# mLSTM input projection: the low halves of sixteen weight blocks formed on the vector engine instead of GpSimd

## The chip, the cores and the metric

The kernel runs on one core of one Trainium2 chip. The metric is the device time of one execution in microseconds; the shown time of the kernel before is the median of 3 runs, 1545.17 us (1545.28, 1542.12 and 1545.17). The engines of the core each run their own in-order queue of instructions: TensorE (PE in the profile, with its weight loads under PEld), the vector engine (DVE), the scalar engine (ACT), GpSimd (POOL) and SyncE (SP, which only issues transfers).

## The reference

Two layers of a backbone work on 1024 latent tokens and 128 context tokens of width 1024. Layer 0 runs four mLSTM heads in both directions beside grouped-query attention, from one input projection; layer 1 is neighbourhood attention. Only the projection of layer 0 and the mLSTM heads matter here:

```python
p = jnp.einsum('btd,dn->btn', h, w_in)
qa, ka, va, oa, gates, qb, kb, vb, z = jnp.split(p, offsets(EVEN_SIZES), axis=-1)
...
h_f, C_f, n_f, m_f = mlstm_scan(qa, ka, va, ig_f, fg_f, *st_fwd)
h_b, C_b, n_b, m_b = mlstm_scan(rev(qa), rev(ka), rev(va), rev(ig_b), rev(fg_b), *st_bwd)
ha = rmsnorm(h_f + rev(h_b), g_hn.reshape(H_A, 1, DH_A)) * jax.nn.sigmoid(oa.astype(jnp.float32))
...
y = jnp.concatenate([ha, from_heads(hb)], axis=-1) * jax.nn.silu(z)
```

Each head has five column blocks of 128 in `w_in`: q, k, v, o and z.

## The kernel before

All products with float32 weights are done as three products of a reduced-width type. A weight block `raw` (128 x 1024, eight 128 x 128 tiles side by side) is loaded by SP, ACT rounds it to the high part `whi` (line 114), and the low part is the difference `wlo = raw - whi` (line 115, in the helper `split`). `feat` then multiplies a block with one chunk of 384 tokens: 24 matmuls (8 tiles, and for each `whi` with the high activations, `whi` with the low ones, `wlo` with the high ones: lines 366 to 368) that add up in one bank of PSUM. The banks of this kind (`pj`) are two. When a chunk is done its bank is emptied by ACT or DVE: q and v by copies (`qT`, `vT`, lines 101 and 103), k by ACT (line 584), o by ACT (lines 603 and 604), z by ACT and DVE (lines 390 and 391, then 610).

Four blocks of head 0 are projected in the front of the kernel, while the inputs are normalised. Their low parts are formed on DVE already. The sixteen others pass through `blocks`, which calls `weights` and `feat` block by block: the z block of head 0, and q, k, v, o and z of heads 1 to 3. `blocks` runs between the pieces of the mLSTM heads, so that TensorE has projections of the next head to do while one head's chain goes on. That chain is: state updates (`kw` on ACT line 662, the product in the single bank `o` line 665, the update of the state tiles `cs` on DVE line 672), the decay matrices `e` (ACT line 649, GpSimd line 650, DVE lines 698 and 703), the products with values and states (lines 709 and 711), the norm of the result (ACT 717, DVE 720 and 721, ACT 724, DVE 725, ACT 728, GpSimd lines 133 and 134, ACT 732), the transposes on TensorE (line 106) and the gate on DVE (line 743).

Between these the generator `rest` (`mods_rest`) computes the modulation vectors of the later sub-layers on DVE: 32 loads `wm` of 512 KB and for each four multiply-and-sum instructions (`mj<-wm,cb`, line 253, 128 x 512), 128 in all.

The order of the instructions on each engine is not the order of the code: the program is built with a scheduler that plays the program through a timeline of its own and places each instruction when its operands would be ready there (`schedule_with_timeline_sim=True`, line 1628). Only in the attention stages is TensorE's order fixed by hand. After that each engine's queue is fixed and runs in order, an instruction waiting at the head of its queue holds up all behind it.

Of the kernel before, what the change touches and what calls it, by code (L numbers as in the profile page):

```python
# [39 lines left out]
class Kern:  # L40
# [1246 lines left out]
    def run(self):  # L1287
        nc, a = self.nc, self.a
# [2 lines left out]

        def blocks(hd, evs, bs, new=None):
            for b in bs:
                w = self.weights(a["w_ab"][5 * hd + b], new=new)
                for c in range(NC):
                    self.feat(h, w, evs[b], [c])
                    next(rest, None)

        with self.phase("front"):
# [21 lines left out]
            w = [[self.u([P, NB, 256], F32R, n) for n in ("whi", "wlo")] for _ in range(4)]  # L1321
# [52 lines left out]
        with self.phase("a"):  # L1374
            self.gates(gT)
            self.c0 = [self.load_c0(hd) for hd in range(2)]
            self.nall = self.const([P, 8], "nall")
            later(2, (1, 2))
            for b in range(3, NB + 1):
                for c in (1, 2):  # L1380
                    later(c, (b,))
            blocks(0, evs, (4,), lambda n: self.t(n, 1, [P, D], F32R))
            nxt, evs = self.mlstm_proj(1)
            blocks(1, evs, (0, 1))
        with self.phase("mlstm", ("e", 3, [P, 4, CW])):
            self.ts = [self.decays_load(0, g) for g in range(NC)]
            start = self.mlstm_start(0)
            rest = self.mods_rest()
            for hd in range(HA):
                self.mlstm(hd, *start, *pr())  # L1390
                if hd < HA - 1:
                    pr = nxt
                    blocks(hd + 1, evs, (2, 3, 4))
                    start = self.mlstm_start(hd + 1)
                    if hd < HA - 2:
                        nxt, evs = self.mlstm_proj(hd + 2)
                        blocks(hd + 2, evs, (0, 1))
            for _ in rest:
                pass
        with self.phase("g", ("nr", 3, [P, 3, 256])):  # L1400
            w = self.gqa_kv(h, self.zb(h))
            Q, early = [], []
            for g in range(2):
                q, w = self.gqa_q(h, g, w, Q, early)
                Q.append(q)
        gz, w = w, []
# [7 lines left out]
        with self.phase("out0"):  # L1414
            new = lambda: self.t("x", 5, [P, D])
# [32 lines left out]
        with self.phase("na"):  # L1448
# [12 lines left out]
            w, ys, gg = [], [], []  # L1461
# [170 lines left out]
```

## Time and profile before

| | |
|---|---|
| runs before | 1545.28, 1542.12, 1545.17 us; median 1545.17 |
| the profiled execution: its time | 1544.44 us |
| its span, first to last instruction | 1542.7 us |
| mean granted TensorE clock | 0.994 |
| PE busy in the span | 1497.6 us (97%) |
| DVE, ACT, POOL busy | 828.7, 711.1, 487.9 us |
| L115 on POOL, 128 x 1024 | 59 instructions, 145.2 us |
| stretch of the sixteen blocks | low parts formed from 71.0 to 348.7 us |

A row of the timeline gives the start in us from the span's start, the duration in us, the engine, the line, the operation, and output<-inputs by the program's names; in brackets stands how long the engine was idle just before, and whose instruction ended that. A row of the windows gives for each engine its busy time and number of instructions in a stretch, then the granted TensorE clock. A row for a tile or a line gives the least, the median and the greatest duration in ns.

### The profile page before, as it was taken

The page shows a single profiled execution, that of the slowest core. Times are in us where ns is not written, and L with a number is a line of the kernel's source. Part 1 is how long each engine was busy: PE and PEld are TensorE (multiplying, and loading weights), DVE is VectorE, ACT ScalarE, POOL GpSimd, SP SyncE. Part 2 cuts the span into 40 slices and gives each one's busy share as a digit, 9 for nine tenths or more (in the row PEclk, how much of TensorE's full clock was granted, in tenths as well). Part 3 has the DMA queues.
Part 4 walks back from the last instruction along what each step waited for, and adds up shares of the span by engine and source line. Part 5 has one row for each costly group of instructions (what it writes and reads, how often), then busy time and mean ns, then how long its engine had stood idle before and what let it go on. Part 6 is the DMA issues. An engine that isn't in the chain of part 4 may idle for free.

```text
span 1542.7 us, 27090 instructions
## 1 busy us (share of the span) xinstructions
PE 1497.6 (97%) x10139; PEld 1377.5 (89%) x10139; DVE 828.7 (54%) x2371; ACT 711.1 (46%) x1767; POOL 487.9 (32%) x660
## 2 busy tenths in 40 slices
PE   7899999999999899999999999999999999999998
PEld 5799999999999888877888989999999999989886
DVE  5832887954457756665465352435253434445532
ACT  4523524344435767777354352435253434445411
POOL 0102323221235745566123241233132323233200
PEclk9999999999999999999999999999999999999999
DMA  9203536422210000022334122131213021225342
GB/s 381 71 15 117 220 126 221 150 91 89 108 64 29 17 24 32 24 73 67 124 122 151 64 61 79 39 103 34 84 42 101 27 86 47 78 79 165 113 131 82
DMA packets 73284, 143.80 MB, mean 93 GB/s; under 512 B 15737, under 2 KB 44609, under 8 KB 73153
## 3 DMA queue, kind: packets, MB, share of 16 engines
q1 hardware_dynamic: 68566, 126.91, 24.6%
q10 hardware_dynamic: 4586, 15.16, 2.6%
q8 instruction: 80, 1.31, 0.3%
q14 instruction: 52, 0.42, 0.1%
HBM read 115.47 MB, written 21.86 MB: 89 GB/s over the span
## 4 chain that ended last, share of the span: by engine, by line
PE 87%; DVE 6%; ACT 2%; issue 2%; DMA 2%; POOL 1%; SPq 0%; DVEq 0%; POOLq 0%; ACTq 0%
PE pj L366 12%; PE pj L367 12%; PE pj L368 12%; PE pj L381 7%; PE pj L382 7%; PE pj L383 7%; PE s L907 4%; PE o L947 4%; PE ptr L106 4%; PE o L1282 4%; PE tr L106 3%; PE s L1259 3%; PE pj L106 2%; DVE mj L253 2%; DMA wm<-in_w_modT_dram 1%
## 5 line engine op out<-in xcount | busy, mean ns | idle before, releaser
L366 PE MATMUL pj<-hh,whi 128*128 128x384 f32 x1168 | 400.2, 343 | 4.4 <-DVE z L391 2.0
L368 PE MATMUL pj<-hh,wlo 128*128 128x384 f32 x1168 | 397.6, 341 | 0.0
L367 PE MATMUL pj<-hl,whi 128*128 128x384 f32 x1168 | 397.6, 340 | 0.0
L115 POOL TENSOR_TENSOR wlo<-raw,whi 128x1024 fp32r<-128x1024 f32 x59 | 145.2, 2464 | 302.9 <-ACT whi L114 241.8
L366 PEld LDWEIGHTS pj<-hh,whi 128*128 128x128 f32 x1168 | 220.5, 189 | 8.9 <-ACT qT L101 2.5
L367 PEld LDWEIGHTS pj<-hl,whi 128*128 128x128 f32 x1168 | 220.5, 189 | 1.2
L368 PEld LDWEIGHTS pj<-hh,wlo 128*128 128x128 f32 x1168 | 220.3, 189 | 1.0
L1269 POOL TENSOR_SCALAR sb<-sb,sm 128x512 f32<-128x512 f32 (+1 forms) x128 | 84.7, 666 | 246.2 <-DVE sm L1268 242.6
L917 POOL TENSOR_SCALAR pr<-pr,smg 128x384 f32<-128x384 f32 x192 | 109.3, 586 | 81.1 <-PE pj L106 41.5
L381 PE MATMUL pj<-whi,hh 128*128 128x256 f32 x432 | 122.4, 284 | 0.3 <-DVE nr L782 0.3
L382 PE MATMUL pj<-wlo,hh 128*128 128x256 f32 x432 | 122.4, 284 | 0.0
L383 PE MATMUL pj<-whi,hl 128*128 128x256 f32 x432 | 122.3, 283 | 0.0
L908 DVE CUSTOM_DVE_ANT_0 pr<-s,zero 128x384 f32<-128x384 f32 x192 | 103.4, 552 | 25.1 <-PE s L907 21.7
L381 PE MATMUL pj<-whi,yh 128*128 128x512 f32 x288 | 114.2, 397 | 1.5 <-DVE o L1077 1.5
L382 PE MATMUL pj<-wlo,yh 128*128 128x512 f32 x288 | 113.8, 395 | 0.0
L383 PE MATMUL pj<-whi,yl 128*128 128x512 f32 x288 | 113.4, 394 | 0.0
L1267 ACT ACTIVATE sb<-sb,sm 128x512 f32<-128x512 f32 (+1 forms) x128 | 88.9, 695 | 52.7 <-DVE sm L1265 49.1
L253 DVE CUSTOM_DVE_ANT_0 mj<-wm,cb 128x512 f32<-128x512 f32 x128 | 108.8, 850 | 4.1 <-DMA wm<-in_w_modT_dram 2.0
L907 PE MATMUL s<-Kst,Q 128*128 128x384 f32 x384 | 107.5, 371 | 0.7 <-DVE smg L908 0.7
L114 ACT CAST whi<-raw 128x1024 fp32r<-128x1024 f32 x77 | 79.7, 1045 | 19.5 <-DMA raw<-in_w_v_dram 6.7
L1265 DVE CUSTOM_DVE_ANT_1 sb<-s,bias 128x512 f32<-128x512 f32 (+1 forms) x112 | 72.9, 664 | 25.2 <-PE ptr L106 12.6
L381 PEld LDWEIGHTS pj<-whi,hh 128*128 128x128 f32 x432 | 81.3, 188 | 1.4 <-issue 0.5
(346 smaller groups left out, 2887.9 us busy)
## 6 DMA issues: line engine op xcount, KB each, us to landing
wm<-in_w_modT_dram SPq DMA_DIRECT2D x32, 512.0 KB, 5.9
raw<-in_w_c_dram SPq DMA_DIRECT2D x25, 512.0 KB, 3.5
raw<-in_w_ab_dram SPq DMA_DIRECT2D x20, 512.0 KB, 3.6
e<-rbd ACTq DMA_DIRECT2D x12, 768.0 KB, 6.5
bias<-in_na_bias_dram SPq DMA_DIRECT2D x16, 576.0 KB, 5.0
wm<-in_w_mod_dram SPq DMA_DIRECT2D x16, 512.0 KB, 10.0
raw<-in_w_out_dram SPq DMA_DIRECT2D x16, 512.0 KB, 3.5
y<-yd SPq DMA_DIRECT2D x18, 448.0 KB, 3.4
```

Source lines behind the costliest of these rows:

```text
L106: self.nc.tensor.transpose(out, in_, self.ident)
L115: (eng_lo or nc.gpsimd).tensor_tensor(lo, src, hi.bitcast(F32), ALU.subtract)
L253: nc.vector.tensor_tensor_reduce(junk, w[:, b, :], cb[:, r, :], 1.0, 0.0, ALU.mult, ALU.add, mp[:, hf, q // 4, 2 * (q % 4) + b, r : r + 1])
L366: nc.tensor.matmul(ps[:, :CW], a, hh, start=k == 0, stop=False)
L367: nc.tensor.matmul(ps[:, :CW], a, hl, start=False, stop=False)
L368: nc.tensor.matmul(ps[:, :CW], b, hh, start=False, stop=k == KB - 1)
L381: nc.tensor.matmul(ps[:, :width], hh, a, start=k == 0, stop=False)
L382: nc.tensor.matmul(ps[:, :width], hh, b, start=False, stop=False)
L383: nc.tensor.matmul(ps[:, :width], hl, a, start=False, stop=k == KB - 1)
L907: nc.tensor.matmul(s[:, :CW], x, y, start=part == 0, stop=part == 1)
L908: nc.vector.tensor_tensor_reduce(pr[:, c, :], s[:, :CW], zero, -1.0, -NEG, ALU.add, ALU.min, m3[:, c : c + 1])
L917: nc.gpsimd.tensor_scalar(pr[:, c, :], pr[:, c, :], r, 0.5, ALU.mult, ALU.mult)
```

## The change

`blocks` passes `"lo"` to `weights`, so that line 115 goes to DVE for the sixteen blocks that `blocks` handles. Other users of `split` are as they were. (The four blocks of z for the attention heads and the weights of later stages have their own calls.)

```diff
         def blocks(hd, evs, bs, new=None):
             for b in bs:
-                w = self.weights(a["w_ab"][5 * hd + b], new=new)
+                w = self.weights(a["w_ab"][5 * hd + b], "lo", new=new)
                 for c in range(NC):
                     self.feat(h, w, evs[b], [c])
                     next(rest, None)
```

As the scheduler sets the order anew, not only these sixteen instructions move. Three places show how.

First, DVE's queue where the front ends: the last low activations `hl` are done, the gates begin (`rows`, `line`), and the first of the sixteen blocks is prepared. `qT_577` empties the bank `pj_903` of head 0's q. Before and after in one piece:

```order
 L474 MEMSET line_772 1x8
 L477 COPY line_772<-sm_775 1x4 x2
+L115 TENSOR_TENSOR wlo_1100<-raw_1097,whi_1099 128x1024
 L103 COPY qT_577<-pj_903 128x2x16x8
 L414 TENSOR_TENSOR gT_165<-pj_744,cross_761 16x2x16x8
```

The low part now stands between the two small copies and the emptying of the bank.

Second, DVE's queue in the chain of state updates of head 1 (`cs_2003` and `cs_2004` are the two directions' states, `o_2271` and the like the products that they wait for, `wlo_2494` the low part of a block of head 2). Before:

```order
L672 SCALAR_TENSOR_TENSOR cs_2004<-cs_2004,astb,o_2263 128x129
L103 COPY k_2214<-ptr_2220 128x384
L253 ISA mj_1690,mp<-wm_2230,cb_1693 128x512
L253 ISA mp 128x1
L672 SCALAR_TENSOR_TENSOR cs_2003<-cs_2003,astb,o_2271 128x129
L672 SCALAR_TENSOR_TENSOR cs_2004<-cs_2004,astb,o_2271 128x129
L253 ISA mj_1690,mp<-wm_2230,cb_1693 128x512
```

With the change:

```order
L672 SCALAR_TENSOR_TENSOR cs_2003<-cs_2003,astb,o_2271 128x129
L672 SCALAR_TENSOR_TENSOR cs_2004<-cs_2004,astb,o_2271 128x129
L103 COPY k_2214<-ptr_2220 128x384
L115 TENSOR_TENSOR wlo_2494<-raw_2491,whi_2493 128x1024
L253 ISA mj_1690,mp<-wm_2230,cb_1693 128x512
L253 ISA mp 128x1
L672 SCALAR_TENSOR_TENSOR cs_2003<-cs_2003,astb,o_2279 128x129
```

The update that stood behind the first `mj` stands ahead of it, and the next update has the low part and one `mj` ahead of it.

Third, GpSimd's queue in head 1's norm (`sm_2357` and `sm_2417` are the reciprocal roots of two groups of chunks, `e_2363` the decay matrices of the next head):

```order
 L133 TENSOR_SCALAR sm_2357<-sm_2353 128x3
 L134 TENSOR_TENSOR sm_2357<-sm_2357,mhalf 128x3
-L650 AFFINE_SELECT e_2363<-e_2363 128x384
-L115 TENSOR_TENSOR wlo_2723<-raw_2720,whi_2722 128x1024
 L133 TENSOR_SCALAR sm_2417<-sm_2413 128x3
```

The second root follows the first without the low part (and without one of the two selections of the decay matrices, which went ahead) between them.

## The prediction

> **What bounds the kernel now.** I read the page first, then the windows over the stretch in which the sixteen blocks are prepared, then TensorE's waits there, and last the timeline around each of those waits.
>
> ```profile
> PE 1497.6 (97%) x10139; PEld 1377.5 (89%) x10139; DVE 828.7 (54%) x2371; ACT 711.1 (46%) x1767; POOL 487.9 (32%) x660
> ```
> ```profile
> 160.00:300.00 140.00, 134.36 (x842) 130.16 (x841) 123.48 (x324) 61.60 (x192) 44.88 (x41) 1.00 0.50 176
> 300.00:350.00 50.00, 49.96 (x330) 49.21 (x329) 32.44 (x93) 21.71 (x72) 13.21 (x13) 1.00 0.33 121
> 350.00:440.00 90.00, 90.00 (x588) 89.56 (x587) 34.89 (x89) 33.56 (x106) 16.36 (x29) 1.00 0.25 91
> ```
> TensorE bounds the kernel: it is busy for 97% of the span. The change can only win what TensorE idles or loses in clock in its stretch. From 160 to 300 us TensorE is idle for 140.00 - 134.36 = 5.6 us, and this is also where DVE is fullest, 123.5 of 140 us. From 300 to 440 us there is nothing left to win. Behind that, TensorE has no slack that would swallow a gain: what it wins here moves the end.
>
> ```profile
> PE pj L366 <- DVE z L391: 2.0, 2, 1.4
> PE pj L366 <- ACT qT L101: 2.0, 2, 1.6
> PE tr L106 <- ACT hs L732: 1.7, 2, 1.0
> PE s L711 <- DVE cs L672: 1.1, 1, 1.1
> PE o L665 <- DVE cs L672: 0.2, 1, 0.2
> ```
> These are TensorE's waits from 60 to 350 us. The longest six behind 150 us are two for z, one and one for the states cs, two for hs: 2.0 + 1.1 + 0.2 + 1.7 = 5.0 us. So I looked at what each of the late instructions stood behind.
>
> ```profile
> 279.85 2.91 POOL L115 TENSOR_TENSOR wlo<-raw,whi 128x1024 fp32r<-128x1024 f32 x1 [1.50 <-ACT whi L114]
> ...
> 280.84 2.47 DVE L253 CUSTOM_DVE_ANT_0 mj<-wm,cb 128x512 f32<-128x512 f32 x1
> ...
> 283.24 0.54 DVE L391 SCALAR_TENSOR_TENSOR z<-th,pj 128x384 f32<-128x384 f32 x1
> ...
> 283.84 0.44 PE L366 MATMUL pj<-hh,whi 128*128 128x384 f32 x1 [1.37 <-DVE z L391]
> ```
> ```profile
> 233.58 2.39 POOL L115 TENSOR_TENSOR wlo<-raw,whi 128x1024 fp32r<-128x1024 f32 x1 [21.21 <-ACT whi L114]
> ...
> 233.74 2.78 DVE L253 CUSTOM_DVE_ANT_0 mj<-wm,cb 128x512 f32<-128x512 f32 x1
> ...
> 236.45 0.60 DVE L672 SCALAR_TENSOR_TENSOR cs<-cs,astb,o 128x129 f32<-128x129 f32 x2
> 236.84 0.49 PE L711 MATMUL s<-cs,e 128*128 128x129 f32 x2 [1.09 <-DVE cs L672]
> ```
> This is the point of the case. Whenever GpSimd forms a low part, a multiply-and-sum of DVE that overlaps it takes 2.5 to 2.8 us and ends about half a us behind GpSimd's instruction. Its usual time is 0.69 us:
>
> ```profile
> L253 DVE CUSTOM_DVE_ANT_0 mj<-wm,cb x103: 643/691/2924, 159.9 to 299.5; 128x512 f32<-128x512 f32 x103
> L253 DVE CUSTOM_DVE_ANT_0 mj<-wm,cb 128x512 f32<-128x512 f32 x103 | 89.4, 868 | 3.6 <-DMA wm<-in_w_modT_dram 2.0
> L115 POOL TENSOR_TENSOR wlo<-raw,whi x9: 2386/2657/2941, 166.1 to 295.2; 128x1024 fp32r<-128x1024 f32 x9
> L115 DVE TENSOR_TENSOR wlo<-raw,whi x18: 1214/1224/1992, 19.5 to 1420.6; 128x1024 fp32r<-128x1024 f32 x18
> ```
> The first three rows are of 160 to 300 us, the last of the whole span. So DVE is not only busy there, it stands: 103 x (0.868 - 0.691) = 18.2 us of its 123.5 are spent in instructions that wait for GpSimd, and the z or the state behind them makes TensorE wait.
>
> The two waits for hs pass through GpSimd's own queue:
>
> ```profile
> 264.34 2.94 POOL L115 TENSOR_TENSOR wlo<-raw,whi 128x1024 fp32r<-128x1024 f32 x1 [4.70 <-ACT whi L114]
> ...
> 267.37 0.52 POOL L133 TENSOR_SCALAR sm<-sm 128x3 f32<-128x3 f32 x1
> ...
> 268.92 1.28 POOL L134 TENSOR_TENSOR sm<-sm,mhalf 128x3 f32<-128x3 f32 x1
> ...
> 270.23 0.99 ACT L732 ACTIVATE hs<-hs,sm 128x128 f32<-128x128 f32 x3 [2.84 <-POOL sm L134]
> ...
> 270.69 0.33 PE L106 MATMUL tr<-cc,hs 128*128 128x128 f32 x1 [0.96 <-ACT hs L732]
> ```
> The root of the norm stands behind a low part on GpSimd, ACT waits 2.84 us for it and TensorE 0.96.
>
> **The change part by part.** (1) *The first block, 71 to 75 us.*
>
> ```profile
> 71.02 3.21 POOL L115 TENSOR_TENSOR wlo<-raw,whi 128x1024 fp32r<-128x1024 f32 x1 [11.13 <-ACT whi L114]
> ...
> 72.07 2.18 DVE L477 COPY line<-sm 1x4 f32<-1x4 f32 x1
> ...
> 74.18 0.15 DVE L477 COPY line<-sm 1x4 f32<-1x4 f32 x1
> 74.25 0.41 DVE L103 COPY qT<-pj 128x256 f32<-128x256 f32 x1
> ...
> 74.69 0.27 ACT L101 COPY qT<-pj 128x128 f32<-128x128 f32 x1 [1.09 <-DVE qT L103]
> 75.00 0.45 PE L366 MATMUL pj<-hh,whi 128*128 128x384 f32 x1 [1.57 <-ACT qT L101]
> ```
> A copy of four numbers takes 2.18 us, because GpSimd is at its low part; the bank is emptied late and TensorE idles 1.57 us. With the change DVE does the two copies (its twin behind takes 0.15 us) from 72.07 to about 72.37, the low part until 73.59 (1.22 us; `whi` was ready by 71.02, when GpSimd began), and the bank at 73.59 instead of 74.25. TensorE starts 0.66 us earlier: **-0.7 us**, and its gap shrinks to 0.9.
>
> (2) *The clock.* Behind that gap TensorE loses half its clock:
>
> ```profile
> 72.67:76.09 3.42, 1.85 (x12) 1.25 (x11) 2.51 (x5) 0.74 (x2) 1.56 (x1) 1.00 0.22 40
> 76.09:82.91 6.82, 6.82 (x27) 6.31 (x27) 0.57 (x3) 0.00 (x0) 0.00 (x0) 0.50 0.14 57
> ```
> 6.82 us at 0.50 cost 3.4 us. The stretch ahead has TensorE busy for 1.85 of 3.42 us. The gap of 1.37 us at 283 us was not followed by a slower clock (the window above shows 1.00 from 160 to 300). With 0.9 us of gap I take the clock to stay full: **-3.4 us**; the bounds are 0 and -3.4. The three runs before, two near 1545.2 and one at 1542.1, are 3.1 us apart, which is near this price; so I count it as part of the median.
>
> [...]
>
> (3) *The nine blocks from 160 to 300 us.* DVE loses 18.2 us of standing and gains 9 x 1.22 = 11.0 us of work, each piece placed by the scheduler and half as long as the old stall. If TensorE's waits go with DVE's lost time, 7.2 of 18.2, or 40%, of the 5.0 us go: -2.0 us. If the waits came only because the stalls were long, all go: -5.0 us. A bank needs emptying while the other fills, and 24 matmuls take about 24 x 90.00/588 = 3.7 us by the row of 350 to 440 us; a low part and an `mj` ahead of a bank, 1.9 us, fit into that, and the old 2.8 us with what stood before them did not. At GpSimd the root loses 2.9 us of queue, but DVE's new low part can stand ahead of the norm's own steps. I take **-3.5 us**.
>
> (4) *The other six.*
>
> ```profile
> L115 POOL TENSOR_TENSOR wlo<-raw,whi x16: 2367/2490/3215, 71.0 to 346.3; 128x1024 fp32r<-128x1024 f32 x16
> ```
> Of the sixteen, one is the first block and nine are those of (3). Three of the others lie between 80 and 160 us and three behind 300 us, and TensorE's list of waits has next to nothing there: 6 x 1.22 = 7.3 us, half of it on a DVE that is idle 17.6 of 50 us from 300 to 350. **0**, covered by that idleness; without the cover at most 0.275 us of waiting per us (5.0/18.2), 2.0 us.
>
> (5) *What is queued behind.* Before, GpSimd waited for `whi` and nothing was hurt. Now DVE waits for it, with the emptying of banks and the state updates behind.
>
> ```profile
> 292.59 0.69 DVE L253 CUSTOM_DVE_ANT_0 mj<-wm,cb 128x512 f32<-128x512 f32 x1
> ...
> 294.10 1.03 ACT L114 CAST whi<-raw 128x1024 fp32r<-128x1024 f32 x1
> ...
> 298.35 0.55 DVE L103 COPY qT<-pj 128x384 f32<-128x384 f32 x1
> ```
> In the new order the low part of this block follows an `mj` that ended at 293.28, and `whi` was done at 295.13: a wait of 1.9 us. Behind it stands a bank of q that was emptied only at 298.35, so even here nothing is late: 295.13 + 1.22 + one `mj` of 0.7 is 297.1. I laid the other blocks onto the old times in the same way. The last, at 346 us, would wait for `whi` too, where TensorE has other work, and the one at 198 us would, but there the new order of ACT has the cast earlier. **0.** No transfer is added; the buffer `raw` is free 1.2 us sooner.
>
> The sum: -0.7 - 3.4 - 3.5 = -7.6 us. On the profiled execution (1544.44 us, span 1542.7 and 1.7 around it) that is 1536.8; the median of the runs is 0.7 higher, so **1537.5 us**.
>
> **The rivals.** *The clock stays slow* (0.20). For it: in the same span other gaps are followed by full clock and by half clock, so the tie between gap and clock rests on one place. Against: it starts within 1.1 us of the gap's end. Time: 1545.17 - 0.7 - 3.5 = 1541.0.
>
> *The waits come back* (0.15). DVE stays near full, the low parts stand ahead of z and the states, and TensorE waits as before, only elsewhere: 1545.17 - 0.7 - 3.4 = 1541.1 with the clock full, 1544.5 with it slow. For it: two thirds of the freed time is refilled. Against: pieces of 1.22 us instead of 2.8.
>
> *DVE waits for the casts: slower* (0.10). The low part is at the head of DVE's queue while ACT, with its own queue of norm and evacuation, has not rounded the block. If each of the nine waited 1.9 us as at 293 us, DVE would stand or work 9 x 3.1 = 28.1 us in place of 18.2; at 0.275 us per us TensorE waits 7.7 instead of 5.0, and a gap of over 1.57 us costs another 3.4 of clock: 1545.17 - 0.7 + 2.7 + 3.4 = 1550.6. It decides once the mean wait for `whi` is over 18.2/9 - 1.22 = 0.8 us. Against: the new order of ACT puts some of these casts earlier.
>
> **How the numbers follow.** The forecast has 0.55, the rivals 0.20, 0.15 and 0.10. About 0.2%, 3.1 us, is what a measurement of this kernel can tell from no change, so faster means under 1542.1. The forecast counts there in full, the slow clock (1541.0, spread 1.7) with 0.14, the returning waits with 0.05: faster 0.74. Same: 0.06 + 0.10 = 0.16. Slower 0.10. The forecast's own range is 1534 to 1541: all five us of waits gone is 1536.0, and another clock loss more or less is worth 1.7 to 3.4; to hold 8 in 10 it reaches up to the two middle rivals: 1534 to 1544.
>
> **What would show it.** Right: no `mj` over 1.5 us from 160 to 300 us; 16 low parts on DVE of 1.22 us; TensorE's idle time there down from 5.6 to about 2; the gap near 75 us under 1.0; the clock at 1.00 from 76 to 83. Wrong: rows of DVE idle before L115 with ACT's `whi` as the releaser and TensorE waiting for z or cs; or the half clock at 76 us behind a gap under 1 us.

## The result and the profile after

The changed kernel takes **1535.1 us** (median of 6 executions, 1533.06 to 1537.54), beside 1544.69 us for the kernel before (6 executions, 1541.54 to 1547.32): a ratio of 0.9944, with a 95% interval of 0.9931 to 0.9958. That is 9.6 us faster. The profiled execution was the slowest of the six, 1537.54 us with a span of 1535.8, so what the two traces differ by (6.9 us of span) is less than what the medians differ by.

The windows of the changed kernel, over the stretches that the prediction looked at. A row has the stretch, its length, then busy time and instructions of PE, PEld, DVE, ACT and POOL, the granted clock, the DMA share and GB/s:

```profile
60.00:80.00 20.00, 17.98 (x104) 15.93 (x103) 14.10 (x44) 9.53 (x24) 0.00 (x0) 1.00 0.08 27
...
140.00:160.00 20.00, 17.85 (x105) 16.76 (x106) 9.21 (x24) 4.68 (x12) 0.00 (x0) 0.91 0.27 106
160.00:300.00 140.00, 139.45 (x889) 138.13 (x889) 123.88 (x356) 62.82 (x194) 23.30 (x32) 1.00 0.54 189
```

From 160 to 300 us TensorE is idle for 0.55 us where it was 5.6, while DVE is as full as before, 123.9 us instead of 123.5. From 60 to 80 us the half clock is gone. In exchange there is a slower piece, clock 0.91, from 140 to 160 us, which the prediction did not foresee.

TensorE's waits from 60 to 350 us, and the two groups of DVE that the change is about (least, median and greatest duration in ns; the multiply-and-sums are those of 160 to 300 us, the low parts those of 60 to 350):

```profile
PE pj L366 <- ACT qT L101: 1.2, 2, 0.8
PE s L709 <- DVE e L703: 1.1, 2, 0.8
PE pj L408 <- DVE hl L325: 0.8, 1, 0.8
PE ptr L106 <- ACT k L101: 0.6, 1, 0.6
PE s L711 <- DVE cs L632: 0.5, 1, 0.5
PE pj L368 <- DVE wlo L115: 0.4, 1, 0.4
PE ptr L106 <- ACT kT L584: 0.3, 1, 0.3
```
```profile
L253 DVE CUSTOM_DVE_ANT_0 mj<-wm,cb x111: 650/691/998, 159.3 to 299.8; 128x512 f32<-128x512 f32 x111
```
```profile
L115 DVE TENSOR_TENSOR wlo<-raw,whi x16: 1206/1222/1540, 72.1 to 337.2; 128x1024 fp32r<-128x1024 f32 x16
```

No wait for z, for hs or for a state of line 672 is left. The multiply-and-sums that took up to 2.9 us are all under 1.0 us, and the low parts on DVE have the 1.22 us that was reckoned with.

How much that is worth is better read from equal work than from equal times. The same 1251 matmuls, found in both traces by their place in the program (one record is missing in the second), before and after:

```profile
149.10:351.70 202.60, 196.92 (x1251) 191.87 (x1250) 161.99 (x435) 87.93 (x281) 59.90 (x57) 1.00 0.46 164
```
```profile
148.34:343.16 194.82, 194.15 (x1250) 192.38 (x1250) 156.78 (x447) 89.50 (x283) 29.75 (x45) 1.00 0.48 171
```

They take 194.8 us instead of 202.6: **7.8 us less**. The idle time of TensorE falls by only 5.0 (5.68 to 0.67); the other 2.8 us come out of its busy time (196.9 to 194.2), with the same matmuls in it. In two further profiles of the changed kernel (`e0_again`, `e10_after`) the same matmuls take 7.3 and 8.0 us less than in the kernel before.

How far the change runs ahead of the kernel before, at the same matmul: 0.1 us at 61 us; 0.9 us at 75 us; 3.7 us at 83 us, as the clock is full; 0.8 us at 149 us, since 2.9 us are lost between 138 and 149 us; 8.6 us at 346 us; 9.0 us at 734 us; 6.7 us at 1431 us. The last loss, 2.2 us near 1410 to 1430 us, lies behind a transfer (ACT waits 3.96 us for `y` until 1417.72); the other two profiles of this kernel have 0.4 and 0.8 us of it, and of the two profiles of the kernel before one loses 2.2 us more there than the other, so it isn't the change's.

### The profile page after: what moved, and what is told of

The parts are those of the page before. It is cut to its first block, busy times and chain, and to the rows that moved or that the text cites. A ratio compares the mean times of both kernels' runs of the same rounds, so it can differ in the third digit from the quotient of the medians.

```text
span 1535.8 us, 27072 instructions
## 1 busy us (share of the span) xinstructions
PE 1493.2 (97%) x10139; PEld 1375.7 (90%) x10139; DVE 825.7 (54%) x2387; ACT 712.5 (46%) x1767; POOL 448.6 (29%) x644
## 4 chain that ended last, share of the span: by engine, by line
PE 49%; DMA 1%; DVE 1%; ACT 1%; POOL 1%; issue 1%; DVEq 0%; POOLq 0%
PE pj L366 7%; PE pj L367 7%; PE pj L368 7%; PE pj L382 6%; PE pj L381 6%; PE pj L383 6%; PE o L1282 4%; PE s L1259 3%; PE ptr L106 2%; PE tr L106 2%; DMA y<-yd 1%; DMA raw<-in_w_out_dram 1%; POOL wlo L115 0%; PE o L947 0%; DVE sb L1265 0%
## 5 line engine op out<-in xcount | busy, mean ns | idle before, releaser
L115 POOL TENSOR_TENSOR wlo<-raw,whi 128x1024 fp32r<-128x1024 f32 x43 | 103.0, 2400 | 133.0 <-ACT whi L114 115.7
L253 DVE CUSTOM_DVE_ANT_0 mj<-wm,cb 128x512 f32<-128x512 f32 x128 | 89.3, 697 | 5.1 <-DMA wm<-in_w_modT_dram 2.8
```

What stands on the lines that cost most here:

```text
L115: (eng_lo or nc.gpsimd).tensor_tensor(lo, src, hi.bitcast(F32), ALU.subtract)
L253: nc.vector.tensor_tensor_reduce(junk, w[:, b, :], cb[:, r, :], 1.0, 0.0, ALU.mult, ALU.add, mp[:, hf, q // 4, 2 * (q % 4) + b, r : r + 1])
```

## The experiments

The theory on record: GpSimd's low part makes DVE stand, and what DVE then empties late makes TensorE wait. Its size was in doubt (2.0 to 5.0 us of waits, and whether the clock at 76 us follows the gap), and the rivals were that the clock stays slow, that the waits come back, and that DVE waits for the casts. Each kernel's time stands beside the kernel before on the same chip, whose median was 1544.68 on the chip of the first four, 1542.2 on that of the second four, and 1541.87 on the last.

### One part at a time

`e1_first` moves only the first block (z of head 0); `e2_heads` leaves the first three of the sixteen on GpSimd and moves the other thirteen; `e3_both` moves all but q and k of head 1; `e0_again` is the change.

```diff
-                w = self.weights(a["w_ab"][5 * hd + b], "lo", new=new)
+                w = self.weights(a["w_ab"][5 * hd + b], "lo" if hd == 0 else "", new=new)            # e1_first
+                w = self.weights(a["w_ab"][5 * hd + b], "lo" if 5 * hd + b > 6 else "", new=new)      # e2_heads
+                w = self.weights(a["w_ab"][5 * hd + b], "lo" if 5 * hd + b not in (5, 6) else "", new=new)  # e3_both
```

> Only the first of the sixteen blocks (z of head 0) has its low part on the vector engine; the other fifteen stay on GpSimd. My theory (the stall of DVE behind GpSimd at 72 us makes the gap of 1.57 us, and the gap costs the clock): the gap falls to about 0.8 us, the half clock from 76 to 83 us is gone, TensorE is 0.7 + 3.4 = 4.1 us ahead at 90 us, and nothing is won after that: ratio about 0.9975 (1540.6 us). Rival (the clock has another cause): the gap shrinks, the half clock at 76 us stays, 0.7 us: ratio 0.9995. Rival (the whole gain comes from the new order of the heads): no change.

> The thirteen blocks from v of head 1 on have their low parts on the vector engine; the first three stay on GpSimd. My theory: the stalls of DVE from 160 to 300 us are gone and with them about 5 us of TensorE's idle time there, while the gap of 1.57 us at 75 us stays and in the profiled execution the half clock behind it is likely: ratio about 0.9968 (1539.7 us). Rival (waits follow DVE's work, of which 40% goes): 2 us, ratio 0.9987. The second part of the theory is that the 2.3 us lost from 138 to 150 us in the changed kernel come from the order that the blocks q and k of head 1 bring with them: then they are not lost here.

> The first block and the thirteen from v of head 1 on are on the vector engine, the blocks q and k of head 1 (the low parts at 85 and 122 us) on GpSimd. If the loss of 2.3 us from 138 to 150 us in the changed kernel comes with these two blocks, the gains add: 4.1 + 5.0 with nothing lost, ratio about 0.9930 and TensorE's idle time from 130 to 160 us as before. If it comes from the order of the heads in general, it is there again and the kernel is as fast as the changed one, ratio 0.9944.

> The changed kernel once more, beside the three variants: ratio 0.9944 (0.993 to 0.996) as in its first runs. [...] The loss of 2.1 us near 1420 us of its first profile follows a late transfer of y; if that is chance, it is not there again.

| kernel | time, us | ratio to before, 95% interval |
|---|---|---|
| first block alone | 1542.1 | 0.9985 (0.9976 to 0.9993) |
| thirteen blocks of the heads | 1534.91 | 0.9948 (0.9935 to 0.9962) |
| all but q and k of head 1 | 1534.59 | 0.9939 (0.9927 to 0.9952) |
| the change again | 1534.41 | 0.9941 (0.9929 to 0.9954) |

The thirteen blocks bring 9.8 us where 4.9 had been expected for them, and where the prediction had -3.5 us for the heads. The first block alone brings 2.6 us (1.1 to 3.7), between the 4.1 of the prediction and the 0.7 of the rival in which the clock stays slow. The two do not add up: 9.8 + 2.6 would be 12.4, the whole is 10.3. With an uncertainty of over 1 us on each this may be chance, but the traces point to something that both comparisons count.

In its trace the kernel of the thirteen blocks does the matmuls from 149 to 352 us in 8.0 us less than the kernel before, where the medians differ by 9.8. It keeps the first low part on GpSimd, so the gap of 1.56 us at 75 us is still there, and the stretch ahead of 75.6 us is as empty as before; yet its clock stays full. In the trace of the first block alone TensorE wins 3.7 us between 61 and 83 us against the traced kernel before, 0.75 at the gap and 2.95 by the clock, and is 3.2 us ahead at the end. So a loss of clock that the kernel before has in some executions can stand in both gains. Windows of the thirteen blocks, and of the kernel before in a second profile (`e7_before`, below); the first row of each pair is the 3.41 us just ahead of the second, and in the kernel without a slow piece there the pair was laid a whole number of such stretches ahead of its next one:

```profile
72.18:75.59 3.41, 1.85 (x11) 1.46 (x9) 2.91 (x5) 0.74 (x2) 1.96 (x1) 1.00 0.07 13
75.59:82.42 6.83, 6.83 (x44) 6.31 (x43) 0.77 (x5) 1.49 (x3) 0.22 (x1) 1.00 0.20 70
```
```profile
73.49:76.90 3.41, 1.84 (x12) 1.24 (x11) 2.48 (x5) 0.74 (x2) 1.54 (x1) 1.00 0.19 36
76.90:83.72 6.82, 6.82 (x27) 6.31 (x26) 0.57 (x3) 0.00 (x0) 0.00 (x0) 0.50 0.14 59
```

TensorE is busy for 1.85 of 3.41 us in the one and for 1.84 in the other, and only the second is followed by half the clock. So the gap does not bring the half clock each time: it is there behind a gap of 1.56 or 1.57 us in two profiles and not in a third. Behind the gap of 0.81 us none of ten profiles has it (the clock is 1.00 from 60 to 100 us in each).

### The kernel before, profiled once more

> The kernel before, unchanged, once more with a profile. Theory (the half clock at 76 us comes in some executions only): the gap of 1.57 us at 75 us is there again and the clock behind it may as well be 1.00. Rival (the gap brings the half clock each time): 0.50 from about 76 to 83 us again.

The kernel before, unchanged: 1547.2 us, with a mean clock of 0.992. The gap of 1.56 us and the half clock from 76.9 to 83.7 us are both there (the second pair of rows above). By itself this would speak for the rival, that the gap brings it each time; the trace of the thirteen blocks speaks against it. The mean clocks of the executions decide for "some of them": of 52 executions of the kernel before beside these experiments, 11 had a mean clock of 0.994 or less, with a median of 1546.0 us, and the other 41 had 1542.0. Of 32 executions of three kernels with a gap of 0.81 us there (the change, the first block alone, all but q and k of head 1) none had; of the five of the thirteen blocks, which keep the long gap, two had. A low mean clock has other sources too: the variants below have that gap of 0.81 us, and 8 of their 44 executions are at 0.994 or less, 7 of them where low parts are formed twice. The 4.0 us between the two groups are near the 3.4 us of the half clock at 76 us, though of executions without a trace it isn't known where the clock was lost. Taken over all, this loss is worth 11/52 x 4.0 = 0.8 us.

It is not the only loss that the kernel before has in some executions. On the second and the third chip its median (1542.2 and 1541.87) lies within 0.4 us of that of its other executions. On the first the median is 1544.68, and five of the twelve executions with a mean clock over 0.994 take 1544.8 to 1545.7 us as well. What those lose is not known, as none has a trace; the loss near 1420 us, 2.2 us in one of the two profiles and not in the other, is a candidate. So the gains that are measured on the first chip, the 2.6 us of the first block among them, may hold up to 2.5 us of losses that the kernel before shows on this chip above all.

### The same sixteen on GpSimd, in quarters

`e4_quarters` is the kernel before, and GpSimd forms each of the sixteen low parts in four instructions.

```diff
-        (eng_lo or nc.gpsimd).tensor_tensor(lo, src, hi.bitcast(F32), ALU.subtract)
+        for j in range(0, D, 256):     # for the blocks of `blocks` alone
+            (eng_lo or nc.gpsimd).tensor_tensor(lo[:, j : j + 256], src[:, j : j + 256], hi[:, j : j + 256].bitcast(F32), ALU.subtract)
```

> The kernel before, with each of the sixteen low parts still on GpSimd but formed in four instructions of 256 columns. Theory (the length of DVE's stall does the harm): an instruction of DVE that overlaps one piece stands for about a quarter of the old time, so the multiply-and-sums of 160 to 300 us stay under about 1.5 us, and the waits of TensorE for z, cs and qT mostly go. The 1251 matmuls that took 202.6 us before and 194.8 us with the change take 195 to 198, and the time is 1537 to 1540 us. Rival (DVE stands for as long as GpSimd works, in whatever pieces): DVE loses its 18 us as before, TensorE's idle time from 160 to 300 us stays near 5.6 us, and the time is 1543 to 1546 us.

1536.74 us, a ratio of 0.9965 (0.995 to 0.998): 5.5 us faster than before with the low parts still on GpSimd, as the theory had it and against the rival. The gap at 75 us is 0.81 us here too, so the first block's 0.7 to 0.8 us are among them. From 160 to 300 us, the window, then the pieces on GpSimd and the multiply-and-sums on DVE:

```profile
160.00:300.00 140.00, 136.61 (x864) 134.62 (x863) 122.56 (x338) 60.83 (x190) 55.54 (x68) 1.00 0.53 189
```
```profile
L115 POOL TENSOR_TENSOR wlo<-raw,whi x36: 722/1182/1277, 162.2 to 290.4; 128x256 fp32r<-128x256 f32 x36
```
```profile
L253 DVE CUSTOM_DVE_ANT_0 mj<-wm,cb 128x512 f32<-128x512 f32 x108 | 85.0, 787 | 4.0 <-DMA wm<-in_w_modT_dram 2.1
```

A piece takes 0.72 us at the least and 1.18 in the median; a multiply-and-sum takes up to 1.3 us instead of 0.69. At 277.14 us three pieces take 3.03 us together: the first starts 0.14 us ahead of a multiply-and-sum, the two others while one is running, which makes about 1.16 each if the first takes 0.72. The multiply-and-sums beside them take 1.15 and 1.10. So each stands for the other. GpSimd works longer than before (55.5 us against 44.9), and DVE loses less: 108 x (0.787 - 0.691) = 10.4 us instead of 18.2. TensorE's waits there are two:

```profile
PE pj L366 <- ACT gate L603: 2.7, 1, 2.7
PE s L709 <- ACT hb L724: 0.5, 1, 0.5
```
```profile
260.41 1.28 ACT L649 ACTIVATE e<-e,nat 128x128 f32<-128x128 f32 x4 [3.50 <-DMA e<-rbd]
...
261.59 0.47 ACT L603 ACTIVATE gate<-pj 128x384 f32<-128x384 f32 x1
...
262.12 0.44 PE L366 MATMUL pj<-hh,whi 128*128 128x384 f32 x1 [2.66 <-ACT gate L603]
```

The longer one is a bank of o that stands in ACT's queue behind a transfer of the decay matrices: what reads it on ACT starts at 260.41 us, 3.50 us after ACT's last instruction. Six loads `wm` for the multiply-and-sums were issued between 247.85 and 257.37 us; over the whole span the median from issue to landing is 4.8 us for a transfer of the decay matrices (768 KB) and 5.3 for a load `wm` (512 KB). The late row is not one of GpSimd or DVE, but whether these loads made it late, and whether the new order brought the transfers together, isn't shown. Without this wait 0.7 us of idle time are left. So the low part can stay on GpSimd at little cost if its instruction is short. Whether the length of each stall counts or their sum, this run can't tell, since both fell.

### GpSimd's instructions put back beside the change

`e6_load` is the change, and GpSimd forms the difference of the sixteen blocks as well, when DVE has read them, and writes it over the raw weights, where nobody reads it.

```diff
-        (eng_lo or nc.gpsimd).tensor_tensor(lo, src, hi.bitcast(F32), ALU.subtract)
+        (eng_lo or nc.gpsimd).tensor_tensor(lo, src, hi.bitcast(F32), ALU.subtract)
+        if more: nc.gpsimd.tensor_tensor(src, src, hi.bitcast(F32), ALU.subtract)
```

> The changed kernel, in which GpSimd forms the difference of each of the sixteen blocks as well, once DVE has read the block, and writes it over the raw weights, where nobody reads it. The low parts that TensorE reads come from DVE as in the change. Theory (GpSimd's instruction holds DVE): the multiply-and-sums of 160 to 300 us go up to 2.4 to 2.9 us again, TensorE's idle time there rises from 0.5 to 5 us or more, and the time is 1543 us or more, up to 1550, since DVE now has the 19.4 us of low parts and the stalls. Rival (the time was lost because the low parts, or what stands behind them on GpSimd, came late): only the waits for the roots on GpSimd come back, at most 1.7 us, and the time is 1534.5 to 1537 us.

1541.64 us, a ratio of 0.9994 (0.9986 to 1.0003): the whole gain is gone, though every low part that TensorE reads comes from DVE. The window; the multiply-and-sums, the low parts and the gates' products on DVE from 160 to 300 us; and one of the places:

```profile
160.00:300.00 140.00, 134.09 (x841) 130.46 (x840) 128.96 (x325) 60.68 (x190) 44.65 (x41) 1.00 0.49 176
```
```profile
L253 DVE CUSTOM_DVE_ANT_0 mj<-wm,cb 128x512 f32<-128x512 f32 x99 | 83.1, 839 | 7.8 <-DMA wm<-in_w_modT_dram 6.5
L115 DVE TENSOR_TENSOR wlo<-raw,whi 128x1024 fp32r<-128x1024 f32 x9 | 11.3, 1255 | 0.2 <-ACT whi L114 0.2
L610 DVE TENSOR_TENSOR gate<-gate,z 128x384 f32<-128x384 f32 x6 | 5.5, 918 | 0.0
```
```profile
248.73 2.78 POOL L115 TENSOR_TENSOR raw<-raw,whi 128x1024 f32<-128x1024 f32 x1 [13.88 <-DVE wlo L115]
...
249.91 2.15 DVE L253 CUSTOM_DVE_ANT_0 mj<-wm,cb 128x512 f32<-128x512 f32 x1
```

The idle time of TensorE is 5.9 us again, and the long multiply-and-sums are back. Against what was expected, the time stays just under the 1543 us of the theory's lower end, and the waits are mostly not the old ones: the greatest sum is 2.5 us for the low part itself. The rival's 1534.5 to 1537 us falls. Another rival, that GpSimd's work keeps the raw buffers longer and so makes the next casts late, falls as well: DVE's low parts wait 0.2 us in all for the casts there.

The multiply-and-sum of these rows, which reads the two tiles `wm` and `cb`, takes 2.15 us instead of 0.69 and ends at 252.06, 0.55 us behind GpSimd's instruction. And it is not all of DVE that stands: between 249.17 and 249.99, beside the same instruction of GpSimd, DVE empties a bank (line 103) in 0.42 us and makes two copies out of PSUM (line 677) in 0.48, 0.28 us each in the mean, as in the change (0.42 and 0.29). What sets the instructions that stand apart from these isn't settled by the runs.

### The low parts twice on DVE

`e5_twice` is the change with each of the sixteen low parts formed twice on DVE; in `e9_half` eight of them are.

```diff
-        (eng_lo or nc.gpsimd).tensor_tensor(lo, src, hi.bitcast(F32), ALU.subtract)
+        for _ in range(cut):     # 2 for all sixteen (e5_twice), or for the odd ones (e9_half)
+            (eng_lo or nc.gpsimd).tensor_tensor(lo, src, hi.bitcast(F32), ALU.subtract)
```

> The changed kernel, with each of the sixteen low parts formed twice on DVE; the second writes the same numbers again. It adds 16 x 1.21 = 19.4 us of planned work to DVE and no stall, nearly what the stalls took before (18.2 us). Theory (a long, unforeseen stall does the harm, planned work does not): TensorE waits little more, 0 to 2 us, so 1534.5 to 1536.5 us. Rival (waits grow with DVE's lost time, whatever its kind): at the prediction's rate of 0.275 us per us it is 5.3 us more, 1539.7; at 7.8 us per 18.2, as measured, 8.3 us more, 1542.7.

> The changed kernel, with the low part formed twice on DVE for eight of the sixteen blocks (5, 7, 9 and so on to 19) and once for the others: half the added work, 8 x 1.22 = 9.8 us. Forming all sixteen twice added 3.8 us of idle time of TensorE from 160 to 300 us, 1.4 behind it and two slow stretches of the clock. Theory (every microsecond of DVE costs alike there): half of that, 2.6 us of idle time, and 4 to 5 us in all. Rival (DVE has room up to a point, and TensorE waits only beyond it): under 1 us of idle time and under 2 us in all.

Twice for all: 1545.73 us, a ratio of 1.001 (0.9999 to 1.0021). Twice for eight: 1538.92 us, 0.9975 (0.9965 to 0.9984), where the change on the same chip takes 1534.71: 4.2 us more for 9.8 us of added work. Windows of all twice and of half of them, then the low parts of each within them:

```profile
160.00:300.00 140.00, 135.63 (x844) 131.82 (x843) 123.25 (x330) 60.75 (x188) 24.50 (x32) 0.99 0.48 175
```
```profile
L115 DVE TENSOR_TENSOR wlo<-raw,whi x18: 1212/1222/1522, 165.1 to 297.5; 128x1024 fp32r<-128x1024 f32 x18
```
```profile
160.00:300.00 140.00, 137.46 (x869) 134.96 (x868) 123.67 (x347) 61.55 (x190) 23.00 (x32) 1.00 0.53 188
```
```profile
L115 DVE TENSOR_TENSOR wlo<-raw,whi x13: 1212/1217/1220, 166.7 to 290.5; 128x1024 fp32r<-128x1024 f32 x13
```

This was the theory's failure: planned work was to cost next to nothing. It costs as the rival had it and more: the rival's two figures were 1539.7 and 1542.7 us. The trace of twice for all has two pieces of 3.4 us at half the clock behind 200 us, which are worth 3.4 us in it. In idle time of TensorE half the added work costs half as much (2.0 us against 3.8), so there is no room left on DVE in this stretch. Put together, DVE's time from 160 to 300 us in low parts and in standing beside GpSimd (of the multiply-and-sums alone), and the idle time of TensorE there, from one profile each:

| kernel | low parts on DVE, us | standing, us | together | TensorE idle, us |
|---|---|---|---|---|
| quarters on GpSimd | 0 | 10.4 | 10.4 | 3.4, without the transfer 0.7 |
| the change | 9 x 1.22 = 11.0 | about 0 | 11.0 | 0.55 |
| twice for eight | 13 x 1.22 = 15.9 | about 0 | 15.9 | 2.5 |
| before | 0 | 18.2 | 18.2 | 5.6 |
| twice for all | 18 x 1.22 = 22.0 | about 0 | 22.0 | 4.4 |
| GpSimd put back | 11.0 | 99 x (0.839 - 0.691) = 14.7 | 25.7 | 5.9 |

Up to some 10 or 11 us DVE's extra time costs nearly nothing; from there on TensorE waits about 0.4 us per us (2.0 for 4.9, 3.8 for 11.0, 5.4 for 14.7). The kernel before lies 2.5 us above such a line. Of its 5.6 us, 1.7 are the two waits for hs, of which the prediction's rows show that one stood behind a low part in GpSimd's own queue; DVE's time does not count that. Waits for hs are also there with no low part on GpSimd (1.4 us in twice for eight), so this is no more than a candidate. Whether the rest is because its stalls are long, or by where they fall, these runs don't settle: the quarters made the stalls shorter, and their sum smaller too. With GpSimd's instructions put back the gates' products stand as well, 6 x (0.918 - 0.55) = 2.2 us that the table leaves out.

### The other low parts as well

`e8_all` is the change, with the other low parts of weight blocks (633 to 1410 us) on DVE too; `e10_after` is the change beside it.

```diff
-        self.split(hi, lo, raw, eng_hi=nc.vector if vec == "hi" else None, eng_lo=nc.vector if vec == "lo" else None)
+        self.split(hi, lo, raw, eng_hi=nc.vector if vec == "hi" else None, eng_lo=nc.vector)
```

> The changed kernel, with the other 44 low parts of weight blocks (633 to 1410 us) formed on DVE as well. From 360 to 1440 us DVE is busy 550 of 1080 us, and TensorE is idle 18 us, of which one wait of 2.2 us, at 717 us, stands behind two low parts on GpSimd. Theory (DVE has room there, and GpSimd's instructions hold it): that wait shrinks to about 1.3 us like its three twins, a few tenths go elsewhere, and the time is 0.5 to 2 us below the changed kernel's. Rival (the room on DVE isn't where the low parts fall): the emptying of banks stands behind low parts of 1.2 us, and the time is the same or up to 3 us above.

> The changed kernel, unchanged, beside the two others on the same chip. Against the kernel before a ratio of 0.994 to 0.996 as in the two comparisons so far. The theory that the half clock at 145 us comes in some executions only would have it absent at least in one of the three profiles of this kernel; the rival, that the waits of 138 to 146 us bring it each time, has it there again.

1532.97 us, 0.9941 (0.9928 to 0.9954), beside 1534.71 us, 0.9951 (0.9939 to 0.9964), for the change. It is the lowest median of all, 1.7 us below the change, but the intervals overlap: faster isn't shown. TensorE's longest sum of waits behind 350 us, in the change and in this kernel (sum, times, longest):

```profile
PE tr L106 <- POOL pt L1030: 6.2, 4, 2.2
```
```profile
PE tr L106 <- POOL pt L1030: 5.0, 4, 1.3
```

The wait that stood behind two low parts on GpSimd went from 2.2 to 1.3 us, as expected; that is half of the 1.7.

### The loss at 138 to 149 us

TensorE's rows with a wait in the change, and in the kernel that leaves q and k of head 1 on GpSimd:

```profile
140.78 0.71 PE L709 MATMUL s<-v,e 128*128 128x129 f32 x4 [0.32 <-DVE e L703]
...
143.28 0.49 PE L709 MATMUL s<-v,e 128*128 128x129 f32 x2 [0.79 <-DVE e L703]
144.87 0.44 PE L106 MATMUL ptr<-cc,c 128*128 128x128 f32 x2 [0.57 <-ACT k L101]
```
```profile
141.30 0.55 PE L106 MATMUL ptr<-cc,kT 128*128 128x128 f32 x3 [0.57 <-ACT k L101]
...
143.86 0.44 PE L106 MATMUL ptr<-cc,c 128*128 128x128 f32 x2 [0.57 <-ACT k L101]
```

In the change the products with the values wait twice for the decay matrices `e` of line 703; in the other kernel, as in the kernel before, they don't. It is the order and not DVE's load: with GpSimd's instructions put back (`e6_load`) the sixteen low parts are on DVE as well, and the waits for `e` are absent. From 138 to 150 us TensorE's idle time is 2.4 us instead of 1.3, so this costs 1.1 us. A slower piece of the clock follows in the change, 3.4 us at half the clock, so 1.7 us more:

```profile
142.03:145.45 3.42, 1.92 (x12) 1.03 (x10) 1.53 (x3) 1.12 (x2) 0.00 (x0) 1.00 0.00 0
145.45:148.86 3.41, 3.08 (x14) 3.11 (x15) 2.16 (x6) 0.37 (x2) 0.00 (x0) 0.50 0.05 10
```

It is there in two of the three profiles of the change (not in `e10_after`, which has the same waits). In the medians nothing of this shows: the kernel without this loss takes 1534.59 us, the change beside it 1534.41. The ratio of 0.9930 that was expected if the gains add lies within the interval of that kernel, and at the edge of the change's, so the comparison can't decide.

## Why the prediction was right

The time on record, 1537.5 us, is 2.4 us above the measured 1535.1. The direction and the place were right. Two terms of the sum were not, one too large and one too small, and they made up for each other: that the sum came so near is in part luck.

**(1) The gap at 75 us, -0.7: right.** The small copy takes 0.15 us, and TensorE starts 0.9 us earlier, of which 0.1 was there ahead of it:

```profile
72.00 0.15 DVE L477 COPY line<-sm 1x4 f32<-1x4 f32 x1
72.07 1.21 DVE L115 TENSOR_TENSOR wlo<-raw,whi 128x1024 fp32r<-128x1024 f32 x1
...
73.34 0.42 DVE L103 COPY qT<-pj 128x256 f32<-128x256 f32 x1
...
74.12 0.44 PE L366 MATMUL pj<-hh,whi 128*128 128x384 f32 x1 [0.81 <-ACT qT L101]
```

**(2) The clock, -3.4: too much.** In the traced pair it came as foreseen: the lead grows from 0.9 to 3.7 us between 75 and 83 us. What failed is the step "so I count it as part of the median". About one execution in five of the kernel before has a mean clock of 0.994 or less, so on two of the three chips the median is without the loss, and over all executions it is worth 0.8 us. What raises the median on the third is not the clock alone; of the executions whose median was to be predicted the clocks are not on record, other than 0.994 for the profiled one. Half the clock followed gaps of 1.56 and 1.57 us, and never came at 76 us with a gap of 0.81. With the same long gap the loss came in two profiles and not in a third, and the slow stretches shown here last 3.41 or 6.82 us. So the first rival, that the clock stays slow, was wrong for the traced pair and near in the size of this term.

**(3) The nine blocks, -3.5: too little; it is -7.8.** The mechanism was right and two sizes were off. First the idle time: -5.1 us and not -3.5. The lower bound came from a rate drawn through zero, 5.0 us of waits for 18.2 us of standing. The runs show a bend instead: some 10 or 11 us on DVE are free, and the low parts bring just 11.0. So nearly all the waits went, as the upper bound had it, though not for its reason alone: the same bend means that the change has used up DVE's room. Second, the prediction counted a wait by the idle time in brackets. A matmul's row is longer than its place in the stream (rows of 0.34 us start 0.17 to 0.18 us apart), so the first part of a wait is hidden in the row ahead, and the first rows behind it are stretched (0.44 us). The same 1251 matmuls lost 5.0 us of idle time and 2.8 us of busy time, so a count by the idle time alone hides 2.8 of 7.8 us.

**(4) The other six blocks, 0: wrong in one place.** At 138 to 149 us 1.1 us are lost, and 1.7 more where the clock follows. DVE has time there (in the kernel before it is busy for 4.1 of these 11.0 us), so the prediction saw cover; it asked what the low parts cost, and not what the new order does to other instructions.

**(5) DVE's wait for the casts, 0: right.** In the profile it waits in three places, at 119, 319 and 337 us, for 5.2 us in all, and TensorE waits 0.4 us for a low part in one place from 60 to 350 us. Of the two waits that the prediction counted, the last block's came (2.2 us) and the one near 293 us did not. So the rival that ends on the slower side did not come: its condition was a mean wait of 0.8 us over the nine blocks of 160 to 300 us, and there it is 0; over the sixteen it is 5.2/16 = 0.3 us. **The waits come back**, the rival with the price of 1541.1, did not come either, but it was near: with 4.9 us more on DVE in this stretch they do (`e9_half`).

With the sizes that the runs give, -0.7 - 0.8 - 7.8 + 1.1 and up to 1.7 for the clock at 145 us make -6.5 to -8.2. The three comparisons of the medians gave -9.6, -10.3 and -7.2, each uncertain by about 2 us. The changed kernel has nearly the same median in all three (1535.1, 1534.41, 1534.71); it is the kernel before that differs (1544.69, 1544.68, 1541.87). The third agrees with the sum; what the first two have beyond it lies in executions of the kernel before and is not placed.

What the prediction said would show it right: no multiply-and-sum over 1.5 us (0.998 at most), sixteen low parts of 1.22 us, a gap under 1.0 (0.81), full clock from 76 to 83 us, all seen; idle time down to about 2 us, where it is 0.55.

## What to carry to other kernels

Here low parts of 2.4 to 2.9 us on GpSimd, which is busy for 32% of the span, stretched multiply-and-sums of DVE from 0.69 us to as much as 2.92: compare an instruction's greatest duration with its median, and look at what runs beside the long ones. Cutting the long instruction into quarters gave 5.5 us without moving anything, and moving it gave 7.2 to 10.3 on the other chips; but the receiving engine has only so much room, and in this stretch the move filled it, so that 10 us more of work there cost 4 us. Count a wait of TensorE by when the same matmuls start (7.8 us here), not by its idle time (5.0). And before a loss that one profile shows goes into a forecast of the median, look at how many executions have it.

## What the runs showed that was not expected

- With the quarters GpSimd and DVE both lose: a 256-column piece on GpSimd takes 0.72 us at the least and 1.18 in the median, and a multiply-and-sum takes up to 1.30 instead of 0.69.
- Of 7.8 us that TensorE won on equal work, 2.8 were in time shown as busy.
- A stretch of 3.41 us in which TensorE was busy for 1.84 or 1.85 us was followed by half the clock in two profiles and by the full clock in a third; 1.92 of 3.42 us was followed by it as well. What decides between them stays open.
